# A two-layer hybrid decoder trunk on one core: a rebuilt mixer, and every gate/up and gate pair by seven products

## The chip, the core and the metric

The kernel runs on one core of a Trainium2 chip. The metric is the device time of one execution in microseconds (us): the median of three runs, with the lowest and the highest beside it. Engines: PE is TensorE (matmuls), PEld its weight loads, DVE is VectorE, ACT is ScalarE, POOL is GpSimd, SP issues the transfers.

## The reference

`x` is 512 tokens by 1024 features, float32. Two layers follow each other, each made of

```
h = LN(a*h + 0.5*SwiGLU_1(h))          # 1024 -> 2816 -> 1024
h = LN(a*h + W_out(sum of 3 gated branches of h))
h = LN(a*h + 0.5*SwiGLU_2(h))
```

The middle line is the mixer. All its inputs come from one projection of `h`. Branch A is a gated delta rule with 4 heads: short convolution on q, k and v, a lower triangular system per chunk that is solved with a unit triangular coupling matrix, and a scan over the chunks. Branch B is a gated linear unit, a causal depthwise convolution of 31 taps, a LayerNorm, swish and a projection. Branch C is causal attention with low-rank q and kv, 4 heads. Each branch is multiplied by its own sigmoid gate (3 x 1024 columns).

## The kernel before

Everything is float32. A product of two float32 matrices is made of three TensorE products of rounded parts (`mm3`): a high part (a cast on ACT) and a remainder (a subtraction on DVE) of either operand, high x high, high x low, low x high. So each 512 columns of weights cost one ACT cast and one DVE subtraction (`split_into`) before PE can use them. Tokens are columns: 512 at once, or two halves of 256.

Two tiles of 128 output features are a pair, [1024 x 256] weights. `plain()` computes it by 8 x 2 blocks of 512 columns: 48 matmuls. `seven()` cuts weights and x into 2 x 2 blocks and uses seven block products instead of eight: 7 x 4 x 3 = 84 matmuls of 256 columns, and sums of blocks on DVE (`combine`, and one sum per result). `block_sums` makes the sums of x once for each projection. `pair()` takes one or the other by a share: of the 20 pairs of an FFN after the first two tiles (`PLAIN`), 18 go by seven (`FFN_SHARE` 0.9); of a mixer's 12 gate pairs, those from number 4 on (`GATE_FROM`).

The mixer is written in this order: k, q and v of the delta rule with their short convolutions (`short_conv`), the coupling and its inverse, the scan, the latents, the gated linear unit, the output gate, the attention, the taps with their norm (`conv_branch`), then gates and branch outputs. The inverse begins with 31 elimination steps on DVE for the 32x32 diagonal blocks; `spread` writes these to a 128x128 matrix by ACT copies of 32 rows into zeros that POOL wrote; then blocks are doubled to 64 and to 128 by small products on PE with ACT copies between. Of the 31 taps, ACT makes the products of eight and POOL adds them up, DVE does 22 as multiply-adds, and ACT the first.

Nothing runs in the written order. `Planner` records every instruction with an estimated duration and a priority (the PE time recorded so far plus `bias`), and lets each engine take the most urgent instruction whose inputs and buffers are there (`plan`). That gives one fixed order for each engine, which the chip then follows; `window` keeps an instruction from going far ahead of PE. Every instruction is issued from one line, 285, and so the profile has all under L285 and tiles tell them apart: `s` is any of 76 SBUF slots, `raw` weights as they land, `ps` one of 8 PSUM banks, `xh` and `xl` the parts of x, `cst` the statistics of the convolution's norm.

Of the kernel before, what the change touches and what calls it, by code (L numbers as in the profile page):

```python
# [18 lines left out]
T = 512  # L19
# [7 lines left out]
CV_TAPS = 31  # L27
POOL_TAPS = 8
# [8 lines left out]
class Planner:  # L37
    """Records instructions, then issues them in the order of a list schedule:
    an engine takes the most urgent instruction whose operands and buffers are there."""
# [62 lines left out]
    def _cost(self, engine, name, outs, ins, k):  # L102
# [5 lines left out]
        if engine == "PE":  # L108
            if name == "transpose":
                return 116.0  # L110
# [15 lines left out]
        if engine == "ACT":  # L126
            c = (52 if psum else 94) + 0.83 * max(n, 64)
            c += 93 * sum(hasattr(k.get(x), "tensor") for x in ("scale", "bias", "accum_out"))
# [173 lines left out]
FFN_SHARE = 0.9  # L302
GATE_SHARE = 1.0
GATE_FROM = 4
# [3 lines left out]
CONV_BIAS = 60.0  # L308
SUMS_AHEAD = 15.0
# [3 lines left out]
def shape_constants():  # L313
# [11 lines left out]
        "sign": np.where(p % 64 < 32, -1.0, 1.0),  # L325
    }
# [11 lines left out]
def trunk(tc, a, out):  # L338
    pl = Planner(tc)

    with ExitStack() as ctx:
# [29 lines left out]
        # ---------------------------------------------------------- constants  # L371
# [3 lines left out]
        def constants():  # L375
            n = CONSTS.shape[1] - 128
            cst = slot()[:, 0:n]
            Q.dma_start(out=cst, in_=a["consts"][:, 128:])
# [9 lines left out]
        # ------------------------------------------------------------ helpers  # L388
# [40 lines left out]
        def mm3(ps, lh, ll, rh, rl, start, stop):  # L429
            PE.matmul(ps, lhsT=lh, rhs=rh, start=start, stop=False)  # L430
            PE.matmul(ps, lhsT=lh, rhs=rl, start=False, stop=False)
            PE.matmul(ps, lhsT=ll, rhs=rh, start=False, stop=stop)
# [18 lines left out]
        def rsqrt(src, scale, eps, shape, name):  # L451
            """(src * scale + eps) ** -0.5"""
# [120 lines left out]
        def blocks(src):  # L573
            """[1024, 256] as blocks: halves of the rows by halves of the columns."""
# [25 lines left out]
        def seven(src, sums):  # L600
# [8 lines left out]
            def product(w, x):  # L609
                wh, wl = block_split(w)  # L610
                ps = bank()[:, 0:256]
                for k in range(4):
                    mm3(ps, wh[:, k], wl[:, k], x[0][k], x[1][k], k == 0, k == 3)
                return ps
# [27 lines left out]
            # the first tiles, by halves of the tokens  # L642
# [39 lines left out]
        # -------------------------------------------------------------- set-up  # L682
# [62 lines left out]
        # --------------------------------------------------------------- mixer  # L745
        def mixer(l):
# [8 lines left out]
            # ---- gated delta rule: projections, short convolution  # L755
            def short_conv(ps, ft):
# [8 lines left out]
                return t  # L765

# [12 lines left out]
            # per-token log decay and beta, [128 tokens, head, tile]  # L779
# [54 lines left out]
            for h in range(H):  # L834
                G.tensor_tensor(by4(ktok[h]), by4(ktok[h]), fan(rk[:, 4 * h:4 * h + 4], 128), op=MUL)
# [5 lines left out]
            # decay and the coupling within a tile, keys on partitions  # L841
# [3 lines left out]
            for h in range(H):  # L845
# [21 lines left out]
                for b in range(4):  # L867
                    pr = slice(32 * b, 32 * b + 32)
                    G.tensor_tensor(comp3[pr, hu, :], by4(U[h])[pr, :, pr], rep(C("strict")[pr], 4), op=MUL)
            S.activation(kdf, kdf, AF.Exp)  # L870

            for h in range(H):
# [12 lines left out]
                G.tensor_tensor(qf[h], qf[h], egb[h], op=MUL)  # L885
                G.tensor_tensor(by4(ktok[h]), by4(ktok[h]), fan(kdf[:, 4 * h:4 * h + 4], 128), op=MUL)
            for h in range(H):
                w = wcols(C_DV + h * 128)
# [8 lines left out]
            # inverse of the unit triangular coupling: 32-blocks by elimination, then doubling  # L897
# [13 lines left out]

            def zeros(n):
                t = slot()[:, 0:n]
                G.memset(t, 0.0)
# [388 lines left out]
```

## Time and profile before

| | |
|---|---|
| median of three runs | 2505.47 us (2501.07 to 2513.7) |
| span of the profiled execution | 2505.9 us |
| PE busy | 2462.4 us, 98% |
| PE weight loads | 2189.7 us, 87% |
| DVE busy | 2080.9 us, 83% |
| ACT busy | 1179.8 us, 47% |
| POOL busy | 227.0 us, 9% |
| DMA | 267 MB, 107 GB/s |

Read it by stretches: an engine's share over the whole span mixes FFNs and mixers, and a busy PE contains waits, because a matmul's end is modelled. Better for PE is the time from the start of one matmul to the start of the next.

### The profile page before, as it was taken

To read this page: it belongs to the slowest core of one execution; us is meant where nothing else is said; L and a number is where in the kernel's file an instruction comes from. 1 tells how busy PE (TensorE), PEld (TensorE's weight loads), DVE (VectorE), ACT (ScalarE), POOL (GpSimd) and SP (SyncE) were. 2 spreads that over 40 slices of the span, in tenths; PEclk is the share of its full clock that TensorE was granted. 3 is DMA by queue.
4 is the path that set the end of the run, shared out by engine and by line. 5 is a ranking of instruction groups with operands and counts; after the bars stand their busy time and mean duration, and the time that the engine had idled before them with its cause. 6 is when DMAs were issued, how large, how long until landed. Compare 5 with 4: busy or idle time off the path is not lost.

```text
span 2505.9 us, 40419 instructions
## 1 busy us (share of the span) xinstructions
PE 2462.4 (98%) x15284; PEld 2189.7 (87%) x15284; DVE 2080.9 (83%) x4107; ACT 1179.8 (47%) x2477; POOL 227.0 (9%) x214
## 2 busy tenths in 40 slices
PE   8999999999999999999999999999999999999998
PEld 8999888887589989998899998888866898899986
DVE  7999667959899888996589995689689997899964
ACT  5544337365636534443345442273746454445430
POOL 0000003105212000000000000030233020000000
PEclk9999999989899999999999999999989999999999
DMA  5334452222223522334323353521222235333331
GB/s 162 102 108 146 142 147 73 68 69 69 72 80 102 193 86 93 110 108 169 111 93 94 110 161 125 153 61 52 77 84 76 68 110 177 101 93 110 124 137 51
DMA packets 268514, 267.39 MB, mean 107 GB/s; under 512 B 17620, under 2 KB 220320, under 8 KB 268320
## 3 DMA queue, kind: packets, MB, share of 16 engines
q1 hardware_dynamic: 268320, 264.82, 33.8%
q8 instruction: 120, 1.97, 0.3%
q14 instruction: 74, 0.61, 0.1%
HBM read 247.48 MB, written 17.30 MB: 106 GB/s over the span
## 4 chain that ended last, share of the span: by engine, by line
PE 83%; DVE 9%; issue 3%; ACT 3%; DMA 0%; POOL 0%; SPq 0%; DVEq 0%; ACTq 0%; POOLq 0%
PE ps L285 83%; DVE s L285 7%; ACT s L285 3%; DVE mx L285 0%; ACT xh L285 0%; ACT ps L285 0%; DMA s<-in_x 0%; DVE rky L285 0%; DVE rkt L285 0%; DMA s<-trig 0%; DVE ps L285 0%; DVE lrt L285 0%; POOL s L285 0%; DVE xl L285 0%; DVE rs L285 0%
## 5 line engine op out<-in xcount | busy, mean ns | idle before, releaser
L285 PE MATMUL ps<-s 128*128 128x256 f32 (+3 forms) x8444 | 1456.9, 330 | 4.8 <-ACT s L285 3.6
L285 PEld LDWEIGHTS ps<-s 128*128 128x128 f32 (+1 forms) x8444 | 1251.2, 191 | 174.7 <-issue 21.0
L285 PE MATMUL ps<-xh,s 128*128 128x256 f32 (+1 forms) x4192 | 980.1, 321 | 3.2 <-ACT s L285 2.6
L285 PEld LDWEIGHTS ps<-xh,s 128*128 128x128 f32 x4192 | 708.8, 190 | 57.3 <-ACT s L285 2.1
L285 DVE TENSOR_TENSOR s<-raw,s 128x512 fp32r<-128x512 f32 (+1 forms) x844 | 590.1, 725 | 99.2 <-ACT s L285 62.6
L285 PE MATMUL ps<-xl,s 128*128 128x256 f32 (+2 forms) x2096 | 669.6, 320 | 0.6 <-DVE xl L285 0.5
L285 ACT CAST s<-raw 128x512 fp32r<-128x512 f32 (+2 forms) x756 | 438.5, 619 | 247.8 <-PE ps L285 145.1
L285 ACT CAST s<-s 128x512 fp32r<-128x512 f32 (+1 forms) x578 | 327.8, 586 | 442.7 <-DVE s L285 417.6
L285 DVE TENSOR_TENSOR s<-s 128x512 fp32r<-128x512 f32 (+10 forms) x860 | 518.8, 629 | 20.7 <-PE ps L285 11.2
L285 PEld LDWEIGHTS ps<-xl,s 128*128 128x128 f32 (+1 forms) x2096 | 398.9, 190 | 28.1 <-DVE xl L285 1.7
L285 DVE TENSOR_TENSOR s<-ps,s 128x256 f32<-128x256 f32 (+2 forms) x552 | 261.4, 474 | 61.3 <-PE ps L285 49.4
L285 DVE SCALAR_TENSOR_TENSOR s<-s 128x512 f32<-128x512 f32 (+19 forms) x276 | 217.1, 818 | 1.6 <-ACT s L285 1.1
L285 POOL TENSOR_TENSOR s<-s 128x512 f32<-128x512 f32 (+8 forms) x130 | 167.7, 1302 | 433.4 <-ACT s L285 239.2
L285 ACT COPY s<-ps 128x512 f32<-128x512 f32 (+5 forms) x336 | 128.2, 413 | 107.5 <-PE ps L285 97.6
L285 ACT ACTIVATE s<-s 128x512 f32<-128x512 f32 (+6 forms) x194 | 129.1, 689 | 83.6 <-DVE s L285 78.1
L285 DVE SCALAR_TENSOR_TENSOR s<-s,ps 128x512 f32<-128x512 f32 x112 | 75.4, 680 | 108.0 <-PE ps L285 96.0
L285 DVE TENSOR_TENSOR s<-raw 128x512 f32<-128x512 f32 x176 | 120.0, 682 | 0.0
L285 POOL MEMSET s<- 128x512 f32 (+2 forms) x32 | 10.4, 369 | 1146.0 <-PE ps L285 1145.9
L285 PE MATMUL ps<-ident,s 128*128 128x128 f32 (+1 forms) x508 | 82.3, 283 | 25.7 <-DVE s L285 19.8
L285 ACT CAST xh<-ps 128x512 fp32r<-128x512 f32 x48 | 28.5, 593 | 161.9 <-PE ps L285 161.9
L285 ACT ACTIVATE s<-ps,s 128x512 f32<-128x512 f32 x74 | 51.1, 717 | 110.5 <-PE ps L285 110.0
L285 PEld LDWEIGHTS ps<-ident,s 128*128 128x128 f32 (+1 forms) x508 | 62.1, 145 | 45.8 <-ACT s L285 15.3
(103 smaller groups left out, 726.4 us busy)
## 6 DMA issues: line engine op xcount, KB each, us to landing
raw<-in_w_in SPq DMA_DIRECT2D x106, 512.0 KB
raw<-in_ffn_w_gate SPq DMA_DIRECT2D x88, 512.0 KB
raw<-in_ffn_w_up SPq DMA_DIRECT2D x88, 512.0 KB
raw<-in_ffn_w_down SPq DMA_DIRECT2D x88, 512.0 KB
spill<-s SPq DMA_DIRECT2D x40, 256.0 KB
s<-spill SPq DMA_DIRECT2D x40, 256.0 KB
raw<-in_w_out SPq DMA_DIRECT2D x16, 512.0 KB
s<-in_x SPq DMA_DIRECT2D x16, 256.0 KB
```

The costliest lines, as they stand in the source:

```text
L285: self.issued = o["f"](*o["a"], **o["k"])
```

## The change

- `FFN_SHARE` becomes 1.0 and `GATE_FROM` 0: all 20 pairs of an FFN and all 12 gate pairs of a mixer go by seven.
- `seven()` keeps three PSUM banks for the whole pair. Where a block product is to be added to an earlier one, PE goes on accumulating in the bank of the earlier, after ACT has copied out what stands in it. DVE has three sums of 256 columns for a pair, before five and one of 512; ACT has four copies, before one.
- The inverse: after the elimination `spread` is one multiplication by a mask on DVE. Then 128x128 products of whole tiles take the place of the products by blocks: 20 for each head.
- POOL does no arithmetic. Its work goes to DVE, or, where a scale per token is meant, to four ACT instructions of 128 columns (`scale_quarters`).
- The taps: DVE does 30 of 31. The gated linear unit comes before the projection of v, and each tap has a priority of its own, 9 us apart (`CONV_SPREAD`).
- The planner's estimates for PE and ACT are altered, and with them all orders.

```diff
-FFN_SHARE = 0.9
+FFN_SHARE = 1.0
 GATE_SHARE = 1.0
-GATE_FROM = 4
+GATE_FROM = 0
+CONV_AHEAD = 20.0
+CONV_SPREAD = 9.0
...
             if k["rhs"].dtype == F32R:
-                return 2.6 + 213.4 * n / 512 if n >= 256 else 213.0
-            return 4 * 216.0 * max(n, o.shape[0], 88) / 512
+                return 13.4 + n / 2.4
+            part = o.shape[0] < 128 or k["lhsT"].shape[0] < 128
+            return max(8.0 + n / 0.6, 116.0) + (100.0 if part else 0.0)
...
-            c1, c2 = slot(), slot()
-            p1, u = slot()[:, LO], slot()
-            u2, u3 = u[:, LO], u[:, HI]
+            c1, c2, pu = slot(), slot(), slot()
+            p1, u2 = pu[:, LO], pu[:, HI]
+            x, y, z = (bank()[:, 0:256] for _ in range(3))
+            product(x, a11, b11)
+            S.copy(p1, x)
+            product(z, a12, b21)
+            V.tensor_tensor(c1[:, LO], z, p1, op=ADD)
             s1 = combine(a21, a22, ADD)
             s2 = combine(s1, a11, SUB)
-            S.copy(p1, product(a11, b11))
-            V.tensor_tensor(u2, product(s2, t[1]), p1, op=ADD)
+            product(x, s2, t[1], True)
+            S.copy(u2, x)
+            product(y, s1, t[0])
             s3 = combine(a11, a21, SUB)
-            V.tensor_tensor(u3, product(s3, t[2]), u2, op=ADD)
-            p5 = product(s1, t[0])
-            V.tensor_tensor(c2.rearrange("p (a b) -> p a b", a=2), rep(p5, 2),
-                            u.rearrange("p (a b) -> p a b", a=2), op=ADD)
-            V.tensor_tensor(c1[:, LO], product(a12, b21), p1, op=ADD)
+            product(x, s3, t[2], True)
+            S.copy(c2[:, HI], x)
+            V.tensor_tensor(c2[:, HI], y, c2[:, HI], op=ADD)
             s4 = combine(a12, s2, SUB)
-            V.tensor_tensor(c1[:, HI], product(s4, b22), c2[:, LO], op=ADD)
-            V.tensor_tensor(c2[:, LO], product(a22, t[3]), u3, op=ADD)
+            product(y, s4, b22, True)
+            V.tensor_tensor(c1[:, HI], y, u2, op=ADD)
+            product(x, a22, t[3], True)
+            S.copy(c2[:, LO], x)
...
+            def glu_taps(c):
...
+                acc = slot()
+                at = pl.bias
+                for s in range(CV_TAPS):
+                    with pl.stream(bias=at + CONV_AHEAD + CONV_SPREAD * s, window=500.0):
+                        if s:
+                            V.scalar_tensor_tensor(acc[:, s:], t[:, :T - s], w(30 - s), acc[:, s:], op0=MUL, op1=ADD)
...
             for h in range(H):
+                glu_taps(h)
                 w = wcols(C_DV + h * 128)
...
             def spread(c3, h):
-                t = zeros(512)
-                for b in range(4):
-                    pr = slice(32 * b, 32 * b + 32)
-                    S.copy(t[pr, :, pr], c3[pr, 4 * h:4 * h + 4, :])
+                t = slot()
+                four = lambda ap: ap.rearrange("p j (b c) -> p j b c", b=4)
+                V.tensor_tensor(four(by4(t)), c3[:, 4 * h:4 * h + 4].unsqueeze(2).to_broadcast([128, 4, 4, 32]),
+                                four(rep(blocks32, 4)), op=MUL)
...
             for h in range(H):
-                y, x, w, u = spread(y3, h), spread(x3, h), zeros(256), by4(U[h])
...
+                y, x, n = spread(y3, h), spread(x3, h), slot()
+                V.tensor_tensor(by4(n), by4(U[h]), rep(beyond32, 4), op=MUL)
+                f, ft = keep(products(x, n)), keep(products(n, x))
+                V.tensor_tensor(y, y, products(ft, y), op=SUB)
+                V.tensor_tensor(y, y, products(keep(products(f, ft)), y), op=ADD)
                 Y[h] = y
...
-                        if s <= POOL_TAPS:
-                            t = slot()
-                            S.activation(t[:, s:], glu[c][:, :T - s], AF.Copy, scale=w(30 - s))
-                            G.tensor_tensor(accp[:, s:], accp[:, s:], t[:, s:], op=ADD)
...
             def second(m, ps):
                 V.scalar_tensor_tensor(gt[m], gt[m], 1.0, ps, op0=ADD, op1=MUL)
-                G.tensor_tensor(merged[m], merged[m], gt[m], op=ADD)
+                V.tensor_tensor(merged[m], merged[m], gt[m], op=ADD)
```

Three places of the order show what moves. The first is PE at the inverse of layer 1, before; 64x64 and 32x32 are products by blocks, the 512 columns are projections that lie between.

```order
L285 MATMUL ps<-s 64x64 x4
L285 MATMUL ps<-xh,s 128x512 x2
L285 MATMUL ps<-xl,s 128x512
L285 MATMUL ps<-xh,s 128x512
L285 MATMUL ps<-s 32x32
L285 MATMUL ps<-s 64x64 x4
L285 MATMUL ps<-s 32x32 x3
L285 MATMUL ps<-s 64x64 x8
```

The same place in the changed kernel:

```order
L287 MATMUL ps<-xl,s 128x512
L287 MATMUL ps<-xh,s 128x512
L287 MATMUL ps<-s 128x128 x81
L287 MATMUL ps<-ident,lry 128x128 x3
L287 MATMUL ps<-s 128x128 x9
```

The 80 products of the four heads now stand in a row, with no projection among them.

The second is DVE behind the last elimination step (the shuffle of 31 columns and its two operations), before:

```order
L285 STREAM_SHUFFLE s<-s 128x16x31
L285 TENSOR_TENSOR s<-raw,s 128x512
L285 TENSOR_TENSOR s<-s 128x16x31 x2
L285 STREAM_TRANSPOSE s<-s 128x512
L285 TENSOR_TENSOR s<-raw,s 128x512 x6
L285 SCALAR_TENSOR_TENSOR s<-ps,s 128x512
L285 TENSOR_TENSOR s<-raw,s 128x512 x3
L285 TENSOR_SCALAR s<-ps,beta 128x128 x2
```

And in the changed kernel; the eight after the transpose are `spread`, the lengths from 497 to 503 are taps:

```order
L287 STREAM_TRANSPOSE s<-s 128x512
L287 TENSOR_TENSOR s<-s 128x512 x8
L287 TENSOR_TENSOR lrt<-lrt,lrv 128x4
L287 SCALAR_TENSOR_TENSOR s<-s,ps 128x512
L287 TENSOR_TENSOR s<-s,ps 128x512
L287 SCALAR_TENSOR_TENSOR lry<-lrt,lry 128x4
L287 SCALAR_TENSOR_TENSOR s<-s 128x502
L287 SCALAR_TENSOR_TENSOR s<-s 128x500
L287 SCALAR_TENSOR_TENSOR s<-s 128x498
L287 SCALAR_TENSOR_TENSOR s<-s 128x503
L287 TENSOR_TENSOR s<-s,ps 128x512 x2
```

Remainders of weights stood there before; now the inverse's own sums and taps do.

The third is PE within an FFN pair of the changed kernel. Bank 512 is `x` of one pair, 538 that of the next; the wait is for ACT's copy out of bank 512.

```order
L287 MATMUL ps_512<-s_147,s_526 128x256
L287 MATMUL ps_512<-s_148,s_526 128x256
L287 MATMUL ps_512<-s_147,s_527 128x256
L287 MATMUL ps_538<-xh_76,s_541 128x256
L287 MATMUL ps_538<-xl_77,s_541 128x256
L287 MATMUL ps_538<-xh_76,s_542 128x256
L287 MATMUL ps_538<-xh_76,s_541 128x256
L287 MATMUL ps_538<-xl_77,s_541 128x256
L287 MATMUL ps_538<-xh_76,s_542 128x256
L287 MATMUL ps_512<-s_149,s_531 128x256 [waits Activation_49]
```

Before, each product had a bank of its own; here six matmuls of the next pair stand between the end of one product and the next write to its bank.

## Rows read from the trace of the kernel before

**Rows 1.** The page: span; busy us, share of the span and instructions by engine.

```profile
span 2505.9 us, 40419 instructions
PE 2462.4 (98%) x15284; PEld 2189.7 (87%) x15284; DVE 2080.9 (83%) x4107; ACT 1179.8 (47%) x2477; POOL 227.0 (9%) x214
```

**Rows 2.** Timeline of PE in an FFN: start us, us, engine, line, operation, count.

```profile
1039.64 0.62 PE L285 MATMUL ps<-xh,s 128*128 128x512 f32 x2
...
1040.32 0.62 PE L285 MATMUL ps<-xh,s 128*128 128x512 f32 x2
...
1046.90 0.40 PE L285 MATMUL ps<-xh,s 128*128 128x256 f32 x2
...
1047.26 0.40 PE L285 MATMUL ps<-xh,s 128*128 128x256 f32 x2
...
1047.98 0.28 PE L285 MATMUL ps<-xh,s 128*128 128x256 f32 x1
```

**Rows 3.** Windows: stretch, length, PE, PEld, DVE, ACT, POOL busy, clock, DMA share, GB/s.

```profile
520.00:540.00 20.00, 20.00 (x130) 17.51 (x129) 7.17 (x16) 11.82 (x38) 0.62 (x1) 0.50 0.09 21
620.00:630.00 10.00, 4.73 (x13) 1.78 (x12) 9.93 (x17) 3.46 (x9) 5.21 (x4) 0.83 0.29 87
630.00:640.00 10.00, 9.19 (x17) 4.23 (x18) 3.84 (x17) 3.83 (x14) 0.00 (x0) 0.50 0.24 70
700.00:800.00 100.00, 99.61 (x615) 89.35 (x614) 97.26 (x168) 43.79 (x77) 12.83 (x8) 1.00 0.26 80
1000.00:1100.00 100.00, 100.00 (x793) 98.11 (x792) 93.57 (x172) 47.67 (x88) 0.00 (x0) 1.00 0.33 102
```

**Rows 4.** Timeline of DVE: first short-convolution tap, first statistics.

```profile
388.31 0.74 DVE L285 SCALAR_TENSOR_TENSOR s<-ps,s 128x511 f32<-128x511 f32 x1
...
738.08 1.29 DVE L285 BATCH_NORM_STATS2 cst<-ps 128x6 f32<-128x512 f32 x2
```

**Rows 5.** Windows of the mixers' two stretches, layer 1 and 2, columns as in Rows 3.

```profile
388.00:738.00 350.00, 338.83 (x1679) 270.34 (x1678) 300.50 (x643) 194.76 (x514) 88.92 (x77) 0.95 0.23 67
738.00:862.00 124.00, 123.61 (x855) 115.37 (x854) 117.61 (x208) 64.73 (x112) 19.66 (x16) 1.00 0.42 135
1633.00:1977.00 344.00, 332.58 (x1677) 264.90 (x1676) 299.34 (x643) 194.86 (x514) 88.79 (x77) 0.97 0.23 68
1977.00:2101.00 124.00, 123.60 (x856) 115.45 (x856) 117.53 (x207) 64.82 (x112) 19.66 (x16) 1.00 0.42 135
```

**Rows 6.** Timeline of PE: its longest wait in the attention, and a run of 128x128 products.

```profile
630.81 0.45 PE L285 MATMUL ps<-ident,s 128*128 128x128 f32 x1 [6.08 <-DVE s L285]
...
418.43 1.28 PE L285 MATMUL ps<-s 128*128 128x128 f32 x10
```

**Rows 7.** Groups by shape, the inverse's products: count | busy us, mean ns | idle before.

```profile
L285 PE MATMUL ps<-s 128*64 128x64 f32 x192 | 21.5, 278 | 3.1 <-ACT s L285 3.0
L285 PE MATMUL ps<-s 64*64 64x64 f32 x64 | 8.0, 293 | 0.1
L285 PE MATMUL ps<-s 32*32 32x32 f32 x64 | 5.1, 220 | 0.6 <-ACT s L285 0.6
```

**Rows 8.** Timeline of POOL and DVE: POOL's sums, taps beside them, taps alone, remainders.

```profile
605.38 19.83 POOL L285 TENSOR_TENSOR s<-s 128x512 f32<-128x512 f32 x12 [25.49 <-ACT s L285]
...
614.08 6.72 DVE L285 SCALAR_TENSOR_TENSOR s<-s 128x492 f32<-128x492 f32 x4
...
704.71 11.66 DVE L285 SCALAR_TENSOR_TENSOR s<-s 128x495 f32<-128x495 f32 x18
...
886.24 2.48 DVE L285 TENSOR_TENSOR s<-raw,s 128x512 fp32r<-128x512 f32 x4
```

**Rows 9.** Timeline of ACT: the copy out of PSUM behind the matmul of 1047.98; a cast.

```profile
1048.30 0.37 ACT L285 COPY s<-ps 128x256 f32<-128x256 f32 x1 [0.83 <-PE ps L285]
1048.57 0.62 ACT L285 CAST s<-s 128x512 fp32r<-128x512 f32 x1
```

**Rows 10.** Groups by shape, columns as in Rows 7: DVE's sums of 256 columns.

```profile
L285 DVE TENSOR_TENSOR s<-ps,s 128x256 f32<-128x256 f32 x440 | 184.7, 420 | 49.3 <-PE ps L285 37.8 <-ACT s L285 3.4 <-issue 0.5
```

More of the change, by code (lines that the diff above doesn't have):

```diff
@@ L27 @@
 CV_TAPS = 31
-POOL_TAPS = 8
 NOPE, ROPE = 128, 64
@@ L127, in _cost @@
             c = (52 if psum else 94) + 0.83 * max(n, 64)
+            if o.shape[0] < 128 and o.shape[0] % 32 == 0:
+                c += 110
             c += 93 * sum(hasattr(k.get(x), "tensor") for x in ("scale", "bias", "accum_out"))
@@ L325, in shape_constants @@
         "sign": np.where(p % 64 < 32, -1.0, 1.0),
+        "blocks": f // 32 == p // 32,
+        "beyond": f // 32 > p // 32,
     }
@@ L375, in constants @@
         def constants():
-            n = CONSTS.shape[1] - 128
+            n = CONST_COLS["blocks"][0] - 128
             cst = slot()[:, 0:n]
-            Q.dma_start(out=cst, in_=a["consts"][:, 128:])
+            Q.dma_start(out=cst, in_=a["consts"][:, 128:128 + n])
             return lambda name: cst[:, CONST_COLS[name][0] - 128:][:, :CONST_COLS[name][1]]
@@ L427, in split, with mm3 @@
             return h, lo
[L429 to L432, printed above, removed]
+        def mm3(ps, lh, ll, rh, rl, start, stop, more=False):
+            PE.matmul(ps, lhsT=lh, rhs=rh, start=start, stop=False, skip_group_check=more)
+            PE.matmul(ps, lhsT=lh, rhs=rl, start=False, stop=False, skip_group_check=more)
+            PE.matmul(ps, lhsT=ll, rhs=rh, start=False, stop=stop, skip_group_check=more)
         def proj(ps, w, c0=0, c1=T):
@@ L765, in short_conv, with scale_quarters @@
                 return t
+            def scale_quarters(t, cols):
+                for j, q in enumerate(quarters(t)):
+                    S.mul(q, q, cols[:, j:j + 1])
             def squares(ps, out4):
@@ L910, in mixer @@
             Y = [None] * H
-            def zeros(n):
-                t = slot()[:, 0:n]
-                G.memset(t, 0.0)
-                return by4(t)
+            masks = slot()[:, 0:256]
+            with pl.stream(window=40.0):
+                Q.dma_start(out=masks, in_=a["consts"][:, CONST_COLS["blocks"][0]:])
+            blocks32, beyond32 = masks[:, 0:128], masks[:, 128:256]
             def spread(c3, h):
-                t = zeros(512)
-                for b in range(4):
-                    pr = slice(32 * b, 32 * b + 32)
-                    S.copy(t[pr, :, pr], c3[pr, 4 * h:4 * h + 4, :])
+                t = slot()
+                four = lambda ap: ap.rearrange("p j (b c) -> p j b c", b=4)
+                V.tensor_tensor(four(by4(t)), c3[:, 4 * h:4 * h + 4].unsqueeze(2).to_broadcast([128, 4, 4, 32]),
+                                four(rep(blocks32, 4)), op=MUL)
@@ L922, in spread @@
                 return t
             def products(lhs, rhs):
-                m, n = lhs.shape[2], int(np.prod(rhs.shape[2:]))
-                ps = bank()[0:m, 0:4 * n].rearrange("p (j c) -> p j c", j=4)
-                for j in range(4):
-                    PE.matmul(ps[:, j], lhsT=lhs[:, j], rhs=rhs[:, j], start=True, stop=True)
-                return ps
-            def twos(t, b):
-                return t.rearrange("p j (a b c) -> p j a b c", a=2, b=2)[:, :, :, b]
+                ps = bank()
@@ L934, in mixer, with keep @@
+                for p, l, r in zip(quarters(ps), quarters(lhs), quarters(rhs)):
+                    PE.matmul(p, lhsT=l, rhs=r, start=True, stop=True)
+                return ps
+            def keep(ps):
+                t = slot()
+                S.copy(t, ps)
+                return t
             for h in range(H):
-                y, x, w, u = spread(y3, h), spread(x3, h), zeros(256), by4(U[h])
-                uo = by4(slot()[:, 0:256])
-                S.copy(uo.rearrange("p j (a c) -> p j a c", a=2), twos(u, 1))
@@ L939, in mixer @@
-                ps = products(uo, twos(x, 0))
-                for i in range(2):
-                    n = slice(32 * i, 32 * i + 32)
-                    S.copy(w[64 * i + 32:64 * i + 64, :, n], ps[n, :, n])
-                up = products(w, twos(y, 1))
-                a0, a1 = slice(0, 32), slice(32, 64)
-                S.mul(x[a1, :, a0], products(y[a1, :, a1], w[a1, :, a0]), -1.0)
-                for i in range(2):
-                    n, even, odd = (slice(o, o + 32) for o in (32 * i, 64 * i, 64 * i + 32))
-                    S.mul(y[even, :, odd], up[n, :, n], -1.0)
@@ L1057, in mixer @@
             krope = rope(kr, swapped(kr_sb, (0, 0)))
-            glu = []
-            for c in range(4):
-                wa, wb = wcols(C_GLU + c * 128), wcols(C_GLU + 512 + c * 128)
-                pa, pb = bank(), bank()
-                proj(pb, wb)
-                proj(pa, wa)
-                t = slot()
-                S.activation(t, pb, AF.Tanh, scale=0.5, bias=hcol("cv_glu_b", 4 + c))
-                G.tensor_scalar(t, t, 1.0, 1.0, op0=ADD, op1=MUL)
-                V.scalar_tensor_tensor(t, pa, col("cv_glu_b", c), t, op0=ADD, op1=MUL)
-                glu.append(t)
             og = []
```

57 lines of the change are left out of this document (24 added, 33 removed).

## The prediction

> **What bounds the kernel now.** I read the page's head first [rows 1], then PE's pace in a timeline, then windows by stretch, then what PE waits for. PE is busy 98% of the span, but a busy PE hides waits, so its pace counts. In an FFN three matmuls of 512 columns start within 1040.32 - 1039.64 = 0.68 us, 0.2267 each, and three of 256 within 0.36, 0.120 each [rows 2]. The FFN has no hole: PE 100% busy, DVE 94% [rows 3].
>
> The mixers are different. I cut each in two at instructions that both kernels have. Stretch 1 goes from the first short-convolution tap to the statistics of the convolution's norm: 738.08 - 388.31 = 349.8 us in layer 1 [rows 4]; in layer 2 it is the third window, 344 us [rows 5]. Stretch 2 goes from there to the last gated sum: 124 us in either layer [rows 5].
>
> The work in them is counted in the order and priced by rows. PE in stretch 1 has 1048 matmuls of 512 columns (237.6 us), 66 of 256 (7.9), 112 products of 128x128 at 0.224 (25; each is two records, and ten records take (1.28 - 0.27) / 9 = 0.112 each [rows 6]), 159 transposes at a record's 0.11 (17), 64 products of 64 columns and 16 of 32 (17 [rows 7]), and some 9 of attention: 313 us. So 36.8 us are lost in layer 1 and 31 in layer 2. In stretch 2 PE has 641 x 0.120 + 192 x 0.2267 + 2 = 122.5 us: nothing is lost.
>
> Two places lose it. At the inverse PE waits for ACT's small copies and the granted clock is 0.50, the lower level, through 520 to 540 [rows 3]. In the attention PE is busy 4.73 of the ten us from 620 while DVE is busy 9.93, it waits 6.08 us for DVE [rows 6], and at 630 to 640, behind that idle time, the clock is 0.50 again. DVE is late there because POOL works: four taps take 6.72 us, 1.68 each, inside POOL's 605.38 to 625.2, and 18 taps without POOL 11.66, 0.65 each [rows 8]. The Trainium skill (SBUF — State Buffer, Who interferes with whom) calls this an exclusive lock: a DVE instruction with two SBUF inputs fully blocks while a GpSimd one reads SBUF. The trace agrees: POOL's twelve come every 19.83 / 12 = 1.65 us and the taps every 1.68, in turn.
>
> **The change, part by part.**
>
> *Pairs.* A pair costs 48 x 0.2267 = 10.88 us plain and 84 x 0.120 = 10.08 by seven: 0.80 less. In the FFNs 8 pairs change (2 in each of four): **-6.4 us**, all on the path. The 8 in the gates are inside the stretches below. The Trainium skill (TensorE: Matmul & The Clock Gate, Back-to-back issue gap) gives N/2.4 + 2.5 ns, so 109 and 216 ns and by estimate 1.2 us a pair, -9.5 for the eight; [rows 2] show 120 and 227. The sum goes by these.
>
> *New waits in seven.* A bank is written again only when ACT has copied it. Two of the three returns have 12 to 13 matmuls between, over 1.4 us. The third has six: from the start of the last matmul to the next write 0.12 + 6 x 0.12 = 0.84 us. The chain it must cover, from rows: matmul 0.28, ACT starts 0.04 behind it (1047.98 + 0.28 against 1048.30), copy 0.37 [rows 2, 9], and as an estimate another 0.05 back: 0.74. It fits if ACT is free. ACT is busy 48% there [rows 3], mostly with casts of 0.62 us [rows 9]; one just begun outlasts the margin of 0.10 by 0.52, and over all phases of a cast by 0.52 x 0.52 / (2 x 0.62) = 0.22, so 0.48 x 0.22 = 0.10 on average. I take 0 because the chain fits; the other end is 104 pairs x 0.10 = 10 us.
>
> *Inverse on PE.* 160 products of 128x128 at 0.224 are 35.8 us; those removed took 21.5 + 8.0 + 5.1 = 34.6 [rows 7]: about +1, inside stretch 1. Their 80 in a row have no projections to hide waits, but four heads to alternate between.
>
> *POOL's work and the taps on DVE.* DVE's instructions in stretch 1 grow from 611 to 754. A following one starts 0.08 us before the end, so a two-input one of 512 columns counts (2.48 - 0.68) / 3 = 0.60 and not 0.68, a tap 0.645 [rows 8], a sum of 256 columns 0.42 - 0.08 = 0.34 [rows 10]. Before: 150 x 0.602 + 88 x 0.645 + 24 x 0.34 and some 349 others, mostly short-convolution taps, elimination steps and small ones, 103 us: 258. It was busy 300.5 [rows 5], the 42 more being the price of POOL. After: 236 x 0.602 = 142, 120 x 0.645 = 77, 40 x 0.34 = 14, and 358 others, 107: **340 us**. PE after: 884 x 0.2267 + 531 x 0.120 + 192 x 0.224 + 150 x 0.11 + 9 = 333, more than before because gate pairs come ahead of the statistics. So DVE is the longer one. The best share of a long stretch is 97% [rows 3], which gives 340 / 0.97 = 350. But the two do not overlap freely. Counted the same way, up to the scan PE has 180 and DVE 165; from the scan to the statistics DVE has 174.4, at 97% 180, and PE 153. I take the longer of each half, 180 + 180 = **360 us**; the ends are 350, if DVE never pauses, and 378, if it is busy 90%.
>
> In stretch 2 PE has 513 x 0.120 + 166 x 0.2267 + 2 = 101.3 and DVE 86.5 / 0.97 = 89: with the 1.5 us that it has over PE's sum today, 102.8. So layer 1 takes 360 + 102.8 against 349.8 + 124, **-11.0 us**, and layer 2 462.8 against 344 + 124, **-5.2**. What goes: POOL's lock, the wait at 626, most of the half clock. What is late next: DVE from the scan to the statistics, with taps, gate sums and the inverse's sums in one queue.
>
> *ACT* gets 304 instructions more; 328 copies of 0.37 us [rows 9] are 121 us, from 47% to about 52%: hidden, PE or DVE being the longer everywhere. In the FFNs DVE has two sums of 256 columns and one of 512 less in each pair, 1.3 us; that is hidden work and gains nothing.
>
> **Sum**, against the profiled execution: 2505.9 - 6.4 - 11.0 - 5.2 = 2483. Its span stands 0.4 us from the median of the runs, so no correction: **2483 us**.
>
> **Rivals.**
> (a) *DVE runs through.* Stretch 1 takes DVE's 350: 2505.9 - 6.4 - 21.0 - 15.2 = 2463. For it: taps can go at any time now and fill pauses. Against it: the elimination's steps wait for one another, and the softmax chain waits on PE.
> (b) *The stalls stay as large.* The time falls only by PE's work: 6.4 in the FFNs, and in each mixer 435.5 to 434.3: 2497, within the noise. For it: attention and scan are chains, whoever is free; PE's 80 products stand without cover. Against it: the longest wait has POOL behind it [rows 6, 8]. The Trainium skill (Perfetto Trace Analysis, Identifying the Most-Contended Engine) ranks engines by occupancy over the kernel; by it PE at 98% alone would decide, which is this case. [rows 3] speak against it in one stretch: from 620 on DVE is full and PE is not.
> (c) *Slower: DVE becomes the bound of the mixers.* Every share below 90% in stretch 1 loses more than the rest wins: 340 / 0.90 = 378, then 2505.9 - 6.4 + 2 x (378 + 102.8) - 941.8 = 2519. At 88%, 386 us, it is 2535. For it: today DVE is busy 300.5 of 350 there, 86%. Against it: part of that is lack of work (7.17 of 20 us from 520 [rows 3]), which taps will fill.
> (d) *ACT's copies in seven come late*: 10 us as worked out, 2493.
>
> **How the numbers follow.** The forecast has 0.48, (a) 0.19, (b) 0.19, (c) 0.11, (d) 0.03. 0.5% is 12.5 us, about what a measurement can tell from no change: faster means under 2493. The forecast and (a) are faster, 0.67; (b) and (d) are within, 0.22; (c) is slower, 0.11. The range leaves out half of (a)'s lower side and most of (c): 2455 to 2508.
>
> **What would show it.** In the profile after: POOL near 0; taps 0.65 us throughout; matmuls of an FFN still 0.120 apart with no wait for ACT in seven (else d); stretch 1 about 360 and DVE over 93% busy from the scan to the statistics (350 is a; with 375 or more and DVE below 92% it is c); stretch 2 about 103; no wait of PE in the attention over 3 us. Wrong would be the forecast above all if DVE paused in the inverse or the attention while PE waited for it.

## The result and the profile after

The kernel after takes 2465.4 us (median of 4 runs, 2464.4 to 2466.6) against 2505.6 beside it (4 runs), a ratio of 0.9842, 95% interval 0.9821 to 0.9864: 1.6% faster. The profiled executions differ by 2505.9 - 2462.6 = 43.3 us.

The page of after, head, the chain's shares by engine, then the same shares of before:

```profile
span 2462.6 us, 41114 instructions
...
PE 2438.4 (99%) x15860; PEld 2207.6 (90%) x15860; DVE 2044.8 (83%) x4197; ACT 1267.1 (51%) x2781; POOL 0.2 (0%) x4
...
PE 95%; DVE 2%; ACT 2%; issue 0%; DMA 0%; SPq 0%; DVEq 0%; ACTq 0%
```

```profile
PE 83%; DVE 9%; issue 3%; ACT 3%; DMA 0%; POOL 0%; SPq 0%; DVEq 0%; ACTq 0%; POOLq 0%
```

DVE is busy 36 us less in all than in [rows 1], though it took over POOL's work, and its share of the chain falls from 9% to 2%. What PE waits for in after (total, times, longest):

```profile
PE ps L287 <- DVE s L287: 4.7, 5, 2.1
PE ps L287 <- DMA s<-in_x: 4.6, 2, 4.3
PE ps L287 <- ACT s L287: 4.3, 3, 1.8
PE ps L287 <- ACT ps L287: 1.0, 2, 0.5
```

The wait of 6.08 us of [rows 6] is gone, and none in the mixers is over 2.1. Now the two stretches, cut at the marks of [rows 4]: layer 1, its two halves (the scan's first step is at 562), layer 2. Columns as in [rows 3].

```profile
387.18:738.39 351.21, 347.33 (x1973) 291.06 (x1972) 337.33 (x785) 202.86 (x528) 0.00 (x0) 1.00 0.27 75
738.39:839.55 101.16, 101.16 (x696) 94.26 (x695) 88.83 (x171) 61.70 (x118) 0.00 (x0) 1.00 0.44 132
...
1608.29:1960.44 352.15, 348.23 (x1973) 292.56 (x1973) 337.35 (x785) 203.04 (x528) 0.00 (x0) 1.00 0.26 75
1960.44:2061.59 101.15, 101.15 (x696) 94.25 (x695) 88.87 (x170) 61.78 (x118) 0.00 (x0) 1.00 0.44 134
```

```profile
387.00:562.00 175.00, 171.12 (x890) 143.41 (x889) 166.30 (x407) 97.29 (x243) 0.00 (x0) 1.00 0.23 61
562.00:738.00 176.00, 176.00 (x1083) 147.44 (x1081) 170.75 (x380) 105.36 (x287) 0.00 (x0) 1.00 0.30 89
```

Against [rows 5], stretch 1 (up to the statistics of the convolution's norm) is not shorter (351.2 against 349.8 us in layer 1, 352.2 against 344 in layer 2). It holds more of PE's work, and stretch 2 is 22.6 us shorter in either layer, since gate pairs that stood there have moved ahead. The granted clock in stretch 1 was 0.95 and 0.97 and is 1.00. So 43.3 us come as 21.2 in mixer 1, 14.4 in mixer 2, and 7.7 in all the rest.

The mixers' part can be split once more. With the prediction's price for each shape (0.2267 us for 512 columns, 0.120 for 256, 0.112 for a record of 128), the distance from one matmul's start to the next is either that price or more, and what is more is time that PE lost, waiting or at a lower clock (a record that is missing from the trace would count too). From first to last mark, PE's work in a mixer is about 437 us before and 433 after. Its loss is 36 and 30 us before (layers 1 and 2), and 19 and 20 after. So of the mixers' gain of 35.6 us some 27 are lost time that has gone, and only the rest is work that was saved.

Inside stretch 1 the shares change from place to place:

```profile
400.00:425.00 25.00, 23.75 (x124) 19.17 (x124) 17.84 (x59) 24.66 (x79) 0.00 (x0) 1.00 0.24 64
450.00:600.00 150.00, 150.00 (x831) 129.06 (x830) 149.45 (x364) 65.87 (x155) 0.00 (x0) 1.00 0.24 67
620.00:630.00 10.00, 10.00 (x42) 5.42 (x40) 8.88 (x33) 6.49 (x26) 0.00 (x0) 1.00 0.19 49
```

From 450 to 600 PE and DVE are both full, side by side. At 400 to 425 ACT is the full one. What PE still loses in stretch 1 lies near these places: 6 of the 19 us from 375 to 450, 12 from 575 to 650, where scan and attention are; from 450 to 575 it loses almost nothing.

### The profile page after: what moved, and what is told of

The parts are those of the page before. It is cut to its first block, busy times and chain, and to the rows that moved or that the text cites. A ratio compares the mean times of both kernels' runs of the same rounds, so it can differ in the third digit from the quotient of the medians.

```text
span 2462.6 us, 41114 instructions
## 1 busy us (share of the span) xinstructions
PE 2438.4 (99%) x15860; PEld 2207.6 (90%) x15860; DVE 2044.8 (83%) x4197; ACT 1267.1 (51%) x2781; POOL 0.2 (0%) x4
## 4 chain that ended last, share of the span: by engine, by line
PE 95%; DVE 2%; ACT 2%; issue 0%; DMA 0%; SPq 0%; DVEq 0%; ACTq 0%
PE ps L287 95%; DVE s L287 2%; ACT s L287 1%; ACT ps L287 0%; ACT xh L287 0%; DMA s<-in_x 0%; DVE xl L287 0%; DVE lnt L287 0%; DVE lny L287 0%; SPq L287 0%; DVE st L287 0%; DVEq L1293 0%; DVE mv L287 0%; DVE lnv L287 0%; DVE neg_eg L287 0%
## 5 line engine op out<-in xcount | busy, mean ns | idle before, releaser
L287 PE MATMUL ps<-s 128*128 128x256 f32 (+3 forms) x9212 | 1561.3, 324 | 0.0
L287 PEld LDWEIGHTS ps<-s 128*128 128x128 f32 (+1 forms) x9212 | 1351.2, 190 | 154.8 <-issue 17.0
L287 PE MATMUL ps<-xh,s 128*128 128x256 f32 (+2 forms) x4064 | 900.2, 308 | 2.8 <-ACT s L287 1.8
L287 PEld LDWEIGHTS ps<-xh,s 128*128 128x128 f32 (+1 forms) x4064 | 678.2, 191 | 36.5 <-ACT s L287 2.2
L287 DVE TENSOR_TENSOR s<-s 128x512 fp32r<-128x512 f32 (+10 forms) x1014 | 591.3, 612 | 29.1 <-ACT s L287 13.7
L287 ACT CAST s<-raw 128x512 fp32r<-128x512 f32 (+1 forms) x740 | 433.9, 619 | 225.4 <-PE ps L287 162.1
L287 ACT COPY s<-ps 128x256 f32<-128x256 f32 (+3 forms) x664 | 257.4, 400 | 379.8 <-PE ps L287 378.0
L287 PEld LDWEIGHTS ps<-xl,s 128*128 128x128 f32 (+1 forms) x2032 | 387.2, 191 | 17.6 <-DVE xl L287 0.5
L287 DVE SCALAR_TENSOR_TENSOR s<-s 128x512 f32<-128x512 f32 (+26 forms) x356 | 249.7, 712 | 1.4 <-ACT s L287 1.1
L287 DVE TENSOR_TENSOR s<-ps,s 128x256 f32<-128x256 f32 (+1 forms) x336 | 147.5, 439 | 87.9 <-PE ps L287 74.7
L287 ACT ACTIVATE s<-s 128x512 f32<-128x512 f32 x162 | 103.3, 667 | 84.6 <-DVE s L287 83.5
L287 PEld LDWEIGHTS ps<-ident,s 128*128 128x128 f32 (+1 forms) x508 | 61.3, 143 | 36.2 <-issue 12.7
L287 ACT ACTIVATE s<-ps,s 128x512 f32<-128x512 f32 x58 | 40.3, 718 | 45.0 <-PE ps L287 44.6
```

What stands on the lines that cost most here:

```text
L287: self.issued = o["f"](*o["a"], **o["k"])
```

## The experiments

The trace alone leaves two readings. By A, DVE is the longer engine of stretch 1 (as the prediction had it) and the change won by keeping it busy. By B, PE's work sets the time and DVE is cover. Then there is the question which part of the change does it. Ratios are to the kernel before on the same chip; that kernel's median was 2501.3 to 2505.6 us from one set of runs to the next, so differences of a few microseconds between sets are read from ratios and traces.

### Is DVE the bound?

*Fewer taps*: after, with 15 of the 30 DVE taps of a block left out (the convolution is incomplete).

```diff
-                for s in range(CV_TAPS):
+                for s in range(0, CV_TAPS, 2):
```

> The changed kernel with every second convolution tap left out (16 of 31 remain in each of 4 channels, so the convolution is not the reference's). DVE has 60 taps fewer per layer, 60 x 0.645 = 38.7 us; PE's work stays. Theory A (DVE's work sets stretch 1, 351 us of which DVE was busy 337): stretch 1 falls to PE's own 333 us plus what the attention loses, 335 to 342 us, and the kernel to about 2440 us (2435 to 2450). Theory B (PE's work and the chains of the attention and of ACT set it, DVE is only filled up by taps): the two stretches stay within 3 us, kernel 2460 to 2468 us.

Measured: 2469.4 us, ratio 0.9859 (0.9842 to 0.9875). No gain.

The mixer of layer 1 from mark to mark, its two stretches, then the same mixer in after:

```profile
387.74:842.03 454.29, 450.38 (x2666) 386.11 (x2666) 395.35 (x894) 264.48 (x645) 0.00 (x0) 1.00 0.30 88
387.74:706.32 318.58, 314.67 (x1728) 259.40 (x1728) 283.56 (x688) 186.35 (x497) 0.00 (x0) 1.00 0.26 74
706.32:842.03 135.71, 135.71 (x940) 126.71 (x940) 111.79 (x207) 78.12 (x149) 0.00 (x0) 1.00 0.39 120
```

```profile
387.18:839.54 452.36, 448.48 (x2666) 385.31 (x2666) 426.15 (x953) 264.56 (x645) 0.00 (x0) 1.00 0.30 88
```

DVE is busy 31 us less in the mixer, and the mixer is not shorter; PE's loss in it is 21 us, after's 19. So less work on DVE gains nothing, which is B's time, and the prediction's sentence "So DVE is the longer one" falls. What neither theory had: the mark between the stretches moves. The statistics come 32 us earlier, and stretch 2 is 35 us longer. The mark is an instruction of DVE, and PE's work lies before or behind it as the order has it. So between kernels of different order a stretch's length alone says little; the whole mixer counts.

*More of it*: after, with 40 more DVE instructions of 0.60 us in each layer, 24 us a layer, into an array that nothing reads:

```diff
+                spare = slot()
+                for s in range(0, 20, 2):
+                    with pl.stream(bias=at + CONV_AHEAD + CONV_SPREAD * s, window=500.0):
+                        V.scalar_tensor_tensor(spare, t, w(30), t, op0=MUL, op1=ADD)
```

> The changed kernel with ten more DVE multiply-adds of 512 columns per channel, with the taps' priorities, into a tile that nothing reads: 40 x 0.60 = 24 us more of DVE in each layer. Theory A (DVE sets stretch 1): plus 24 us a layer, about 2513 us (2500 to 2516). Theory B (PE and chains): 2463 to 2472 us.

Measured: 2510.3 us, ratio 1.0026 (1.0017 to 1.0036): 45 of the 48 us added come out as time. First two rows of PE's waits, a window of it, and the same window in after:

```profile
PE ps L287 <- DVE lry L287: 13.1, 2, 6.5
PE ps L287 <- ACT s L287: 12.8, 14, 1.8
```

```profile
525.00:575.00 50.00, 38.12 (x181) 32.05 (x181) 45.84 (x107) 10.36 (x18) 0.00 (x0) 0.80 0.07 19
```

```profile
525.00:575.00 50.00, 50.00 (x342) 45.79 (x341) 49.56 (x119) 18.59 (x47) 0.00 (x0) 1.00 0.12 34
```

The time is A's. The end of the elimination (the transpose of the blocks) in after and here:

```profile
545.29 0.70 DVE L287 STREAM_TRANSPOSE s<-s 128x512 f32<-128x512 f32 x1
```

```profile
555.62 0.71 DVE L287 STREAM_TRANSPOSE s<-s 128x512 f32<-128x512 f32 x1
```

22 of the 40 added instructions stand ahead of it, it comes 10.3 us later, and PE's added loss lies at one place: 19.6 us from 525 to 575, where after loses 0.1. There PE waits for the elimination, then for ACT and DVE between the products of the inverse, and the clock falls. So one reading of the two runs is a knee: less work on DVE is worth nothing, and more costs nearly its own length. But the added work had the priorities of every second of the first 20 taps and came to the one place, 450 to 600 us, where DVE is full in after; over after's whole mixer it is busy 426 of 452 us. Whether 24 us at another place would cost as much isn't shown.

### Which part of the change does it?

*Pairs alone*, in three steps on the kernel before, whose mixer, POOL work and estimates stay. First the new seven with every pair by it, in FFN and gates (`seven()` itself is edited as in the change):

```diff
...
-FFN_SHARE = 0.9
-GATE_FROM = 4
+FFN_SHARE = 1.0
+GATE_FROM = 0
...
```

> The kernel before with the new seven() (sums in PSUM) and with all FFN and gate pairs by seven; mixer, POOL's work, taps and planner's estimates as before. Theory A (the rebuilt mixer is what moved the mixers, the pairs are worth PE's 0.80 us each where PE is the bound): 2506 - 6.4 for the FFNs, and the gate pairs add DVE work to a stretch that DVE already fills: 2492 to 2506 us. Theory B (the pairs carry the gain): 2465 to 2480 us.

Measured: 2556.1 us, ratio 1.0198 (1.018 to 1.0216): 2% *slower*, which neither theory had. PE stands once a layer for 19 us behind a run of taps; DVE's queue there (start, duration) and PE's longest wait:

```profile
726.87 19.32 DVE L285 SCALAR_TENSOR_TENSOR s<-s 128x496 f32<-128x496 f32 x30
...
PE ps L285 <- DVE s L285: 20.0, 2, 19.3
```

The before kernel has such a run too, 18 taps at 704.71 [rows 8], but there plain gate pairs with no sums on DVE keep PE busy meanwhile (matmuls of 512 columns throughout, without a pause). To tell the new seven from the gate pairs, the same shares with the *old* seven:

> The kernel before with every pair by seven products in the old way (its own seven, with DVE sums of the products), nothing else of the change: the same pairs as in the run of the new seven on the kernel before, which took 2556. Theory A, it is the pairs that come by seven in the gates that hurt the old mixer, since their sums of weights and of x come on DVE ahead of the statistics while GpSimd slows it: slower as well, 2520 to 2565, with PE waiting 15 us or more for DVE near 725. Theory B, it is the new seven's three banks that hurt: 2488 to 2506 here.

2606.4 us, ratio 1.0398 (1.0383 to 1.0414): A's sign, beyond its range. The new seven isn't what hurts, it is the better of the two by 50 us. By the marks each mixer takes 39 us more than in before, and all the rest 21 more: with the old seven the FFNs lose too. The run of taps is there again:

```profile
751.68 18.68 DVE L285 SCALAR_TENSOR_TENSOR s<-s 128x501 f32<-128x501 f32 x29
```

Last, the new seven with GATE_FROM 4, so that only the FFNs' pairs are added:

> The kernel before with the new seven, and every pair of the FFNs by it; the first four gate pairs of a mixer stay plain as before. Theory A (the gate pairs hurt, not the new seven): the FFNs win 8 pairs x 0.80 = 6.4 us and the mixers, which have four pairs by the new seven, stay, 2494 to 2502. Theory B (the new seven hurts the mixer): 2515 or more. In both PE's loss in the FFNs should be none.

2496.4 us, ratio 0.9973 (0.9961 to 0.9985), 6.8 us of 2502.5, and the mixer of layer 1 takes 472.9 us by the marks against 473.5. The FFNs' term, 6.4, stands, and with the first four gate pairs plain the slow-down is gone: it was these pairs. Then the reverse, the kernel after with the first four gate pairs of a mixer plain again (GATE_FROM 4):

> The changed kernel, but the first four gate pairs of each mixer plain again, as before; FFN pairs all by seven. PE has 4 x 0.80 = 3.2 us more per layer, DVE about 4 x (7.6 - 2.4) = 21 us less per layer (some of it in stretch 1). Theory A (DVE sets stretch 1): stretch 1 gets shorter by up to 15 us a layer, kernel 2440 to 2460 us. Theory B (PE and chains): plus 6.4 us, 2470 to 2474 us.

2472.5 us, ratio 0.9871 (0.9856 to 0.9885): 7 us more than after, 8 pairs at 0.80 are 6.4. So the same eight gate pairs cost 2556.1 - 2496.4 = 60 us in the old mixer and win 7 in the new one. Which part of the new mixer makes this difference isn't shown.

*POOL*: after with eight taps of each block by ACT products and POOL sums again (the first of them begins the second accumulator).

```diff
...
+                        elif 1 < s <= 8:
+                            S.activation(tt_[:, s:], t[:, :T - s], AF.Copy, scale=w(30 - s))
+                            G.tensor_tensor(accp[:, s:], accp[:, s:], tt_[:, s:], op=ADD)
...
+                    V.tensor_tensor(acc, acc, accp, op=ADD)
```

> The kernel after with eight of the 31 taps of each of the four convolution blocks given back to GpSimd: ACT writes a product of 512 columns for each, GpSimd sums them (28 sums of two SBUF inputs a layer, plus the four first ones), and one DVE sum a block joins the two halves. DVE loses 32 taps of 0.645 us and gains 4 sums of 0.60 a layer, 18 us of its own work less. Theory A, GpSimd's lock is what held the mixer of the kernel before: 28 sums of 1.65 us are 46 us a layer in which DVE's two-input instructions take 1.65 to 1.68 us instead of 0.6, so DVE loses about 28 us where it wins 18, and since it has no slack between 430 and 600 us the time rises by about 10 us a layer: 2475 to 2490, GpSimd busy 90 us or more, taps beside it at 1.68. Theory B, the lock is hidden like the rest of DVE's work, PE alone sets the time: within 5 us of after, 2461 to 2471.

Measured: 2553.5 us, ratio 1.0208 (1.0193 to 1.0223). A has the sign, but 88 us is far more than its 10 to 25. From 440 to 560 us, groups of DVE (busy, mean ns of one), of this kernel and then of after:

```profile
L287 DVE TENSOR_TENSOR s<-raw,s 128x512 fp32r<-128x512 f32 x32 | 25.9, 820 | 0.0
L287 DVE SCALAR_TENSOR_TENSOR s<-s 128x503 f32<-128x503 f32 (+8 forms) x25 | 23.2, 932 | 0.8 <-ACT s L287 0.8
```

```profile
L287 DVE SCALAR_TENSOR_TENSOR s<-s 128x511 f32<-128x511 f32 (+15 forms) x55 | 39.4, 729 | 0.0
...
L287 DVE TENSOR_TENSOR s<-raw,s 128x512 fp32r<-128x512 f32 (+1 forms) x34 | 22.6, 673 | 0.0
```

A tap takes 0.93 us on average instead of 0.73, a split 0.82 instead of 0.67. The elimination's end is at 562.9 instead of 545.3. The larger part comes behind it, in the scan. That end, DVE's queue, and PE's wait for it:

```profile
562.88 0.70 DVE L287 STREAM_TRANSPOSE s<-s 128x512 f32<-128x512 f32 x1
...
597.93 16.64 DVE L287 SCALAR_TENSOR_TENSOR s<-s 128x491 f32<-128x491 f32 x26
...
620.09 5.43 PE L287 MATMUL ps<-s 128*128 128x512 f32 x14 [20.75 <-DVE s L287]
...
600.00:625.00 25.00, 4.91 (x13) 3.94 (x14) 25.00 (x41) 1.49 (x3) 0.00 (x0) 0.51 0.06 16
```

The Trainium skill (SBUF — State Buffer, Who interferes with whom) has the lock, and the trace agrees: over the whole kernel the 13 taps that overlap a POOL sum take 1.46 us on average, the other 163 take 0.72. But the most expensive place is one without POOL, whose last sum in layer 1 ends at 534.6: 26 taps in a row, and behind them PE with nothing else to do. The elimination ends 17.6 us late; from there to the scan's last step are 642.2 - 562.9 = 79 us against 585.2 - 545.3 = 40, and in that part no lock is at work: there it is the order of DVE's queue. How much of the first 17.6 is the lock and how much the order isn't shown.

*The taps' place*: after with the gated linear unit and its taps built where before has them, unspread.

> The kernel after with the gated linear unit and its 30 DVE taps a block built where the kernel before has them, behind the short convolutions and the inverse, without the spread, everything else as after. The number of instructions is the same. Theory A, what moved DVE's work ahead (taps that fill the pauses of the short convolution, the inverse and the scan) is what lets DVE run through: DVE then has little to do beside the inverse and too much beside the gates, the statistics of the convolution's norm come 15 us or more later than 738, and the time is 2485 to 2510. Theory B, PE alone sets the time and the place of the taps does not matter, as leaving half of them out did not: 2462 to 2472.

Measured: 2509.4 us, ratio 1.0034 (1.0021 to 1.0047), the upper end of A. The same instructions, and the whole gain is gone. PE's loss in a mixer is 43 and 44 us, after's 19 and 20. DVE's run of taps, PE's wait behind it, and a window at the inverse:

```profile
706.35 16.78 DVE L287 SCALAR_TENSOR_TENSOR s<-s 128x494 f32<-128x494 f32 x26
...
PE ps L287 <- DVE s L287: 14.3, 1, 14.3
...
500.00:545.00 45.00, 45.00 (x313) 41.30 (x311) 36.19 (x75) 14.89 (x39) 0.00 (x0) 1.00 0.17 45
```

DVE pauses beside the inverse (36.2 of 45 us busy, 44.6 in after) and pays at the gates. No run of taps in after is longer than four; here it is 26.

*The inverse*: after with the joining of the 32-blocks as before (zeroed arrays, ACT copies of 32 and 64 rows, small products).

```diff
...
-                f, ft = keep(products(x, n)), keep(products(n, x))
-                V.tensor_tensor(y, y, products(ft, y), op=SUB)
-                V.tensor_tensor(y, y, products(keep(products(f, ft)), y), op=ADD)
...
+                ps = products(uo, twos(x, 0))
+                for i in range(2):
+                    n = slice(32 * i, 32 * i + 32)
+                    S.copy(w[64 * i + 32:64 * i + 64, :, n], ps[n, :, n])
...
```

> The kernel after with the inverse's joining of the 32-blocks as in the kernel before: zeroed arrays, ACT copies of 32 and 64 rows, products of 32 and 64 columns, in place of the whole-array one. DVE is rid of 20 instructions of 0.6 us a layer (12 us), ACT gets 64 small copies in place of 12 large ones, PE's work is about 1 us less. Theory A, the chain of ACT copies is what held the inverse of the kernel before: PE waits for ACT again near 540 to 565 us, the clock falls to the lower level there, and 5 to 15 us a layer are lost: 2475 to 2495. Theory B, the loss there was for want of other work, and the gated linear unit that stands ahead of it now covers it: 2460 to 2470, no half clock.

Measured: 2541.8 us, ratio 1.0141 (1.0124 to 1.0158), far above A. PE's waits at the end of the elimination:

```profile
546.56 1.12 PE L287 MATMUL ps<-ident,lry 128*128 128x128 f32 x4 [9.49 <-DVE lry L287]
567.17 1.09 PE L287 MATMUL ps<-s 128*64 128x64 f32 x8 [19.49 <-ACT s L287]
569.01 2.82 PE L287 MATMUL ps<-s 32*32 32x32 f32 x24 [0.75 <-ACT s L287]
```

A's mechanism, PE waiting for ACT's small copies, is there with 0.75 us. The 19.49 is another: ACT itself waits 28.9 us for DVE's elimination, which ends at 565.1 instead of 545.3. By the trace 70 of the taps with 508 columns or fewer stand ahead of that end, in after 29; 41 taps of 0.645 are 26 us. Why the planner put them there isn't shown. One candidate: the zeroed arrays are written at 352 to 363 us and hold 12 of its 76 buffers until the inverse, and taps are the work on DVE that needs no new buffer. So this run does not price the old inverse; it fits that the order of DVE's queue decides.

*The estimates*: after with the planner's matmul costs of before. The edit also takes back the 110 ns that after's planner adds for an ACT instruction of 32, 64 or 96 rows, so it is all estimates, not PE's alone.

```diff
-                return 109.0
+                return 116.0
...
-                return 13.4 + n / 2.4
...
+                return 2.6 + 213.4 * n / 512 if n >= 256 else 213.0
+            return 4 * 216.0 * max(n, o.shape[0], 88) / 512
...
-            if o.shape[0] < 128 and o.shape[0] % 32 == 0:
-                c += 110
```

> The kernel after, with the planner's estimates of matmul durations as in the kernel before (128 columns at 116 ns, 256 at 109, small ones four times 216 x columns / 512, no extra for narrow outputs); the instructions are the same, only their order differs. Theory A, the order is worth little since PE has other work at nearly every point: within 6 us of after, 2459 to 2471. Theory B, the estimates are a part of the gain, since the small products were taken for longer than they are and the order around the inverse and the attention was wrong: PE loses 10 us or more beyond after, 2475 to 2490.

2478.8 us, ratio 0.9909 (0.9894 to 0.9923): 13 us more than after by the medians, 17 by the ratios, which is B's time. PE's waits for ACT are 12.4 us in 20 places (4.3 in 3 in after). The instructions are the same, so their order under the new estimates is worth about a third of the gain.

### Is ACT hidden everywhere?

At 400 to 425 us ACT is busy 24.66 of 25 us, and PE, by its own pace, loses some 3 us: it starts 72 matmuls of 512 columns, 32 records of 128 and 20 transposes there, 22 us at the prices of the prediction. (The expectation below has 5.3, which these counts don't give.) Two runs relieve it, in place of k's scaling by ACT, and then also of the decay's exponential in quarters:

```diff
-                scale_quarters(ktok[h], rk[:, 4 * h:4 * h + 4])
+                V.tensor_tensor(by4(ktok[h]), by4(ktok[h]), fan(rk[:, 4 * h:4 * h + 4], 128), op=MUL)
```

```diff
-                for j in range(4):
-                    u = 4 * h + j
-                    dj = d[:, j * 128:(j + 1) * 128]
-                    S.activation(dj, dj, AF.Exp, bias=ngc[:, u:u + 1])
+                V.tensor_tensor(by4(d), by4(d), fan(ngc[:, hu], 128), op=ADD)
+                S.activation(d, d, AF.Exp)
```

> The kernel after with the scaling of k by its norms done by four DVE products with a broadcast factor a layer in place of 16 ACT instructions of 128 columns. It relieves ACT at 400 to 425 us, where ACT is busy 24.66 of 25 us and PE loses about 5 us against its pace in either layer. Theory A, ACT is what ends last there: PE's loss at 400 to 425 falls from 5.3 us to under 2 and the time falls by 4 to 10 us, 2455 to 2462. Theory B, the loss only moves (to DVE, which is full from 425 on, or to the attention behind): within 3 us, 2462 to 2469; if DVE's four products delay the scan, 2469 to 2475.

> The kernel after with k's scaling by norms on DVE (four products a layer for 16 ACT instructions, which took 2462.2) and also the decay's exponential in one: four DVE sums with a broadcast row and four ACT instructions of 512 columns in place of 16 of 128 with a bias (16 x 0.39 = 6.2 us against 4 x 0.63 = 2.5). Theory A, ACT's short instructions at 400 to 425 us are what PE's chain still waits for: PE's loss there falls below 2 us a layer and the time to 2455 to 2460. Theory B, what is left there is the chain through DVE: 2460 to 2466.

2462.2 and 2461.7 us, ratios 0.9842 (0.9826 to 0.9859) and 0.9825 (0.9811 to 0.984). PE's waits between 395 and 430, in after and in the first of the two:

```profile
PE ps L287 <- DVE s L287: 2.0, 1, 2.0
PE ps L287 <- ACT s L287: 1.3, 1, 1.3
PE ps L287 <- ACT ps L287: 0.5, 1, 0.5
```

```profile
PE ps L287 <- DVE s L287: 2.9, 3, 1.3
PE ps L287 <- ACT ps L287: 0.5, 1, 0.5
```

The wait for ACT's scaling went and most of it came back as a wait for DVE. From 375 to 450 us PE's loss is 6.4 us in after, 4.9 in the first and 4.7 in the second. By the times it is B, the first at its lower end. The profiled spans are 2.5 and 3.5 us below after's, which the intervals can't tell from nothing. No kernel here beats after for certain.

## Why the prediction was right or wrong, point by point

The time was right in sign and inside the range, 17.6 us below the forecast of 2483, on rival (a)'s 2463. By its steps:

- **Pairs in the FFNs**, -6.4: right. The rest outside the mixers gave -7.7 in the trace, and the run that adds only these pairs 6.8.
- **New waits in seven**, 0: right for the FFNs. Between 862 and 1600 us PE waits 0.4 us in all, for DVE, and its matmuls start 0.120 apart:

```profile
1039.83 0.28 PE L287 MATMUL ps<-xl,s 128*128 128x256 f32 x1
1039.95 0.40 PE L287 MATMUL ps<-xh,s 128*128 128x256 f32 x2
1040.19 0.28 PE L287 MATMUL ps<-xl,s 128*128 128x256 f32 x1
```

- **Stretch 2**, 102.8: measured 101.2 in both layers. Right, 1.6 us high.
- **Stretch 1**, 360: measured 351.2 and 352.2. This term holds 16.6 of the 20.4 us by which 43.3 exceeds the predicted 22.9 (rounded terms). The sums themselves stood: DVE 340 counted, 337.3 busy; PE 333 counted, which with some 19 us lost against its pace (7 up to the scan, 12 behind it) is about the 351. What failed is the cut in two halves. I took "the longer of each half", PE's 180 up to the scan and DVE's 180 behind it. Measured are 175 and 176. By the matmuls that start before 562, PE had 168 of work in the first half, not 180, and so some 164 in the second, not 153: 12 us of its work were put on the wrong side of the scan. With 168 the first half is DVE's 165 at 97%, 170, and the sum 350. That PE loses time of its own, 7 and 12 us, had no term. DVE in the second half was busy 170.75 us, at the 97% assumed, instead of 174.4. Taking the worse engine of each half turned an uncertain boundary into 9 us a layer.
- **DVE is the longer one**: wrong, and the number did not show it. With 31 us less on DVE the mixer took as long. PE's work plus its losses set the mixer's time; that DVE's 350 for stretch 1 came out too does not make DVE the limit. The Trainium skill (Perfetto Trace Analysis, Identifying the Most-Contended Engine), which ranks engines by occupancy, would have had PE here: 99%, its weight loads 90%, DVE 83%. The run with fewer taps agrees; in the one with more DVE work, where the added work was in PE's way at the elimination, 45 us came out as time all the same.
- **ACT hidden, "PE or DVE being the longer everywhere"**: wrong at 400 to 425 us, where ACT is the fullest; for the time it mattered by some 3 us, if at all.
- **What goes** (POOL's lock, the wait at 626, most of the half clock): right. No wait in the attention, the clock at 1.00 there, though PE still runs below its pace:

```profile
630.00:640.00 10.00, 10.00 (x38) 5.24 (x36) 8.81 (x27) 5.03 (x21) 0.00 (x0) 1.00 0.43 136
```

- **Rivals.** (a) had the time, and by the prediction's own sign (350 for stretch 1, DVE over 93% busy behind the scan) it was (a). But it had not the reason: DVE does run through from 450 to 600, yet less DVE work does not shorten the time. (b) fell with PE's waits, 33 us in before and 15 in after. (c) did not come, though it stood close: 24 us more on DVE a layer, or the same taps in another place, give 2509 to 2510. (d) fell with the FFNs' waits.

What the steps did not have is how the parts hang together. I summed pairs, POOL, taps and inverse as if each had a price of its own. The runs give: taps in the old place +44, eight taps on POOL +88, the inverse's old joining +76, old estimates +13, against a whole change of -40. They do not add. What they share is PE's loss: its work in a mixer is 432 to 437 us in every kernel here, its loss from 18 to 78. In four of the slower kernels (both with all gate pairs on the old mixer, the POOL taps, the late taps) a run of 26 or more taps stands on DVE in front of what PE waits 14 to 21 us for. That run and that wait are shown; what makes the planner build it is not.

## What to carry to other kernels

When two engines are both near full in a stretch, price the change by two experiments, some of the second engine's work left out and some added: here the one gave nothing and the other nearly all. Say where in the order the work is added: a second place would have told whether the amount or the place cost the time, and no run here did that. Filler work that can go at any time belongs between other work, one piece at a time: the same 120 taps, moved together with the gated linear unit that feeds them, were worth 44 us in the two layers by their place alone. And a saving on the bound engine (the gate pairs by seven) can cost several times its gain in one surrounding (60 us in the old mixer) and win in another (7 us in the new one), so the order of the edits matters.

## What the runs showed of the hardware

The granted clock was low where PE had stood. Where PE stood for 20.75 us in the run with POOL taps, the stretch of 600 to 625 shows 0.51, about the lower level; with more DVE work 0.80 from 525 to 575; in after stretch 1 is at 1.00 throughout. Before, 630 to 640, behind the wait of 6.08 us, had 0.50; in after both the wait and the low clock are gone there. POOL's lock also reaches the weight splits, whose two inputs lie in SBUF: in the run with POOL taps the 16 splits that overlap a POOL sum take 1.24 us on average, the other 812 take 0.68. In these two kinds it counts little by itself: the 16 splits and the 13 taps are together some 18 us longer, in a kernel that is 88 us slower.
